# A new opening for a backbone kernel: tokens by rows, the modulation map by quarters

## The chip, the cores and the metric

The kernel runs on 1 core of a Trainium2 chip. The metric is the device time of one execution in microseconds (us). Engines: TensorE (PE; PEld are its weight loads), VectorE (DVE), ScalarE (ACT), GpSimd (POOL) and SyncE (SP), whose queue issues the DMAs.

## The reference

Two layers work on 1024 latent tokens (width 1024) and 256 context tokens. The part that matters here is the start of layer 0: both streams are normalised by their root mean square, then scaled and shifted by numbers that come from a map of the conditioning vector, and projected to q, k and v.

```python
mod = silu_c @ w_mod[i] + b_mod[i]          # 1024 -> 6 x 1024
mod_c = silu_cc @ w_mod[i] + b_mod[i]
sh1, sc1, gt1, sh2, sc2, gt2 = jnp.split(mod[:, None, :], 6, axis=-1)
h = modulate(rmsnorm(x, g_attn[i]), sh1, sc1)       # h * (1 + scale) + shift
hc = modulate(rmsnorm(ctx, g_attn[i]), sh1c, sc1c)
q, k, v = attn_inputs(h, w_in, gq, gk, n_kv)        # y = h @ w_qkv, rmsnorm of q and k per head
```

Behind it come neighbourhood attention, an output projection and a gated ConvFFN, and layer 1 with sliding-window attention; the change does not touch these.

## The kernel before

**Layout.** Activations lie with channels on the partitions, as eight blocks of 128 channels (k = 0 to 7), and tokens along a row. The tokens form chunk 0 (latent 0 to 511, tiles 0 to 3 of 128 tokens), chunk 1 (latent 512 to 1023, tiles 4 to 7) and chunk 2 (context, tiles 8 and 9). Products keep fp32 accuracy by splitting both sides in a hi part and a lo part and adding three products: whi x hi, whi x lo, wlo x hi. A projected tile (128 tokens by 384 columns: q, k and v of one pair of heads) therefore takes 8 blocks x 3 = 24 products. The weights of a head pair come as four slabs j of two channel blocks each; ScalarE makes whi, VectorE wlo.

**Order of work.** Nearly every instruction is issued through one helper (line 51, so most rows of the profile say L51). A planner (`Sched`, lines 61 to 223) holds operations with an engine, an assumed duration, what they read and write, a key and buffer counts; it plays them through and lays down one fixed order for each engine. At run time an engine executes its list in that order and waits in place for whatever an instruction still lacks. Two planners follow each other at the start: `sa` for the opening (lines 791 to 936) and `sc` for layer 0's attention (lines 965 to 1232).

**The opening before.** SP loads the context and chunk 0 (x, channels on partitions), then the shift and scale columns of layer 0's map in eight chunks `wm` of 1 MB, one for each block of input channels; the two accumulators `mod` are complete only when the eighth has landed. Then slabs 0 to 2, chunk 1 and slab 3. Meanwhile the sums of squares are made by ScalarE (`sq`) and VectorE (`nsum`), folded over partitions by a product with a column of 1/D (`nps<-invd,nsum`), raised to the power -1/2 by GpSimd, improved by a Newton step on VectorE, and spread again: VectorE makes diagonal matrices `dg`, a product with ones gives the factor for each token on all partitions (`nps<-dg,ones`), and VectorE multiplies x by it. When the map is complete, ScalarE copies it out (`modsb`), TensorE turns it (`modt`), VectorE adds the bias (`modc`), and `apply` makes the hi and lo parts of chunks 2 and 0 (`h0chi`, `h0clo`, `h0hi`, `h0lo`). Chunk 1 waits: `plan_norm` (lines 636 to 724) does its norm inside `sc`, between the first projections, with its lo parts called `n1lo`.

**The attention of layer 0.** For each of eight head pairs, `plan_na_qkv` (line 977) projects the ten tiles in the order 8, 9, 0 to 7 (`mm`, two PSUM banks). Each tile then has a tail: ScalarE copies the bank to `qraw` (two buffers), squares (`qsq`), splits v; VectorE and GpSimd make the factor of the q and k norm (`qv`, `qy`, `qn`), ScalarE and VectorE the hi and lo parts `st`, TensorE turns them into `pt` (four matrices, and `klt`, the lo parts of k, once for two tiles), ScalarE and VectorE copy out q, kk, kl. `plan_na_su` (line 1092) does the attention of two query tiles and a head: scores `s` (context first), an exponential on ScalarE into `S`, a scale, the turn of S into `pt`, its hi and lo parts (`pthi`, `ptlo`), products with v into `pv`.

Of the kernel before, what the change touches and what calls it, by code (L numbers as in the profile page):

```python
# [19 lines left out]
KT = 8  # L20
# [206 lines left out]
def trunk_kernel(ctx, tc, xperm, xseq, cc, wmod, bmod, gnorm, na_wqkv, na_gq, na_gk, na_bias, na_wo,  # L227
# [111 lines left out]
    def t_act(n):  # L339
        return 0.094 + n / 1200.0  # L340
# [452 lines left out]

    with tc.tile_pool(name="x0", bufs=1, reuse_waits="tile") as xp, \
            tc.tile_pool(name="lw0", bufs=2, reuse_waits="tile") as lw, \
            tc.tile_pool(name="ps0", bufs=1, space=PS, reuse_waits="tile") as ps:
        xs = [hpool.tile([P, KT, 512], F32, tag="hhi", name="x0", bufs=2),
              Parts([lo_part("x1", F32) for _ in range(4)], 2),
              Parts([wring.tile([P, 1024], F32, tag="wlo", name="x2").rearrange("p (k t) -> p k t", k=4) for _ in range(2)], 4)]
        h = [hi_lo("h0", 0), None, hi_lo("h0", 2)]  # L800


        sa = Sched(dict(raw=3, w=WBUFS, sq=2, nsum=1, n=2))
        t_mb = 2.45
        for c, parts, key in ((2, 2, 0), (0, 4, 2), (1, 4, 30)):
            t0, n = CH[c]
            for k in range(0, KT, KT // parts):
                def load(e, c=c, parts=parts, k=k, t0=t0, n=n):
                    src = xperm[:, KT * t0 + k * n:KT * t0 + (k + KT // parts) * n].rearrange("p (k t) -> p k t", t=n)
                    dma.dma_start(xs[c][:, k:k + KT // parts, :] if c == 0 else xs[c].tiles[k * parts // KT], src)  # L810
                sa.op("dma", t_mb * n / parts / 256, load, writes=[("x", c, k + i) for i in range(KT // parts)], key=key + k / KT)
# [3 lines left out]
        accs, raws = [None] * 2, [None] * KT  # L815
        for kt in range(KT):
            def load(e, kt=kt):
                raws[kt] = xp.tile([P, 2, 1024], F32, tag="wm", name=f"wm{kt}", bufs=KT)
                dma.dma_start(raws[kt].rearrange("p v c -> p (v c)"), wmod[0, kt * P:(kt + 1) * P, 0:2 * D])

            def mm(e, kt=kt):
                for v in range(2):
                    if kt == 0:
                        accs[v] = ps.tile([P, 512], F32, tag="mod", name=f"mod{v}", bufs=2)
                    mod_mm(accs[v], kt, raws[kt][:, v, :], kt == 0, kt == KT - 1)
            sa.op("dma", t_mb, load, writes=[("wm", kt)], key=4 + kt)
            sa.op("pe", 0.86, mm, reads=[("wm", kt)], writes=[("acc", v) for v in range(2)], key=0)
        for v in range(2):
            J = {}

            def cp(e, v=v, J=J):
                J["sb"] = xp.tile([P, 256], F32, tag="modsb", name="modsb0", bufs=2)
                act.activation(J["sb"], accs[v][:, :256], AF.Copy)

            def tr(e, v=v, J=J):
                J["gen"] = mod_finish(0, v, J["sb"], lambda: ps.tile([P, 512], F32, tag="modt", name="modt", bufs=2))
                next(J["gen"])

            def fin_(e, J=J):
                for _ in J["gen"]:  # L840
                    pass
            sa.op("act", 0.28, cp, reads=[("acc", v)], writes=[("sb", v)], key=-1)
            sa.op("pe", 0.43, tr, reads=[("sb", v)], writes=[("modt", v)], key=-1)
            sa.op("dve", 0.2 + 0.2 * v, fin_, reads=[("modt", v), ("bmod",), ("gn",)], writes=[("modc", v)], key=-1)

        def stats(c, key):

            n = CH[c][1]
            nt = n // P
            J = {}  # L850
            x = xs[c]
            for k in range(KT):
                def sq(e, k=k):
                    J["s", k] = lw.tile([P, 512], F32, tag="sq" if k else "nsum", name="sq" if k else "nsum", bufs=2 if k else 1)
# [4 lines left out]
                sa.op("act", t_act(n), sq, reads=[("x", c, k)], writes=[("sq", c, k)] if k else [("sums", c)], key=key + k,  # L859
                      acq=[("sq", ("sq", c, k), 1)] if k else [("nsum", ("nsum", c), 1)])  # L860
                if k:
                    sa.op("dve", t_dve(n), add, reads=[("sq", c, k), ("sums", c)], writes=[("sums", c)], key=key + k,
                          rel=[("sq", c, k)])

            def mp(e):
                J["mp"] = ps.tile([P, 512], F32, tag="n", name="nps", bufs=2)
                for i in range(nt):
                    pe.matmul(J["mp"][:, i:i + 1], J["s", 0][:, i * P:(i + 1) * P], invd, start=True, stop=True)
            sa.op("pe", 0.22 * nt, mp, reads=[("sums", c)], writes=[("mp", c)], key=key, acq=[("n", ("mp", c), 1)],
                  rel=[("nsum", c)])  # L870

            def v(e):
                for a in "vyt":
                    J[a] = tiny.tile([P, 4], F32, tag="n" + a, name="n" + a)[:, :nt]
                dve.tensor_scalar(out=J["v"], in0=J["mp"][:, :nt], scalar1=EPS, scalar2=None, op0=ALU.add)
            sa.op("dve", 0.08, v, reads=[("mp", c)], writes=[("v", c)], key=key, rel=[("mp", c)], port=False)
# [9 lines left out]
            def dg(e):  # L886
                J["dg"] = lw.tile([P, 512], F32, tag="sq", name="dg", bufs=2)
# [3 lines left out]
            sa.op("dve", 0.2 * nt, dg, reads=[("y", c)], writes=[("dg", c)], key=key, acq=[("sq", ("dg", c), 1)])  # L891

            def bc(e):
                J["bc"] = ps.tile([P, 512], F32, tag="n", name="nps", bufs=2)
                for i in range(nt):
                    pe.matmul(J["bc"][:, i * P:(i + 1) * P], ones, J["dg"][:, i * P:(i + 1) * P], start=True, stop=True)
            sa.op("pe", 0.22 * nt, bc, reads=[("dg", c)], writes=[("bc", c)], key=key, acq=[("n", ("bc", c), KT)], rel=[("dg", c)])
            for k in range(KT):
                sa.op("dve", t_dve(n), lambda e, k=k: dve.tensor_tensor(
                    out=x[:, k, :], in0=x[:, k, :], in1=J["bc"][:, :n], op=ALU.mult),  # L900
                    reads=[("bc", c)], writes=[("x", c, k)], key=key + 8 + k, rel=[("bc", c)], port=False)
# [1735 lines left out]
```

## Time and profile before

| | us |
|---|---|
| median of 3 runs | 2819.89 |
| lowest, highest run | 2819.53, 2821.8 |
| the profiled execution | 2819.35 |
| its span in the profile | 2817.6 |

The span is the time between the first and the last recorded instruction of the one profiled execution; all single durations below come from that execution. A row of the timeline has the start, the duration, the engine, the line, the operation, the tile that is written and those that are read, partitions x elements, the count, and in brackets the idle time of the engine before it and what ended it. Durations of neighbouring instructions overlap, so the cost of one in a row of many is the distance between starts. A plain fp32 product leaves two records, so a count of 8 there can be four products.

### The profile page before, as it was taken

How to read it: one execution, taken by the hardware profiler on the slowest of the kernel's cores; microseconds unless marked ns; L12 is line 12 of the kernel's file. 1: busy time of each engine (PE TensorE's matmuls, PEld its weight loads, DVE VectorE, ACT ScalarE, POOL GpSimd, SP SyncE). 2: the span in 40 equal slices, each digit the busy share in tenths (PEclk: the TensorE clock that was granted, in tenths of full speed). 3: DMA queues.
4: the chain of work that ended last, by engine and by line, in shares of the span. 5: the costliest groups of instructions: out<-in, count | busy, mean ns of one | idle time of the engine just before them, and what ended most of it. 6: DMA issues, size and time to landing. Idle time of an engine off the chain costs nothing. (4 is left out here: it accounts for less than half of the span.)

```text
span 2817.6 us, 45649 instructions
## 1 busy us (share of the span) xinstructions
PE 2758.1 (98%) x16205; PEld 2427.5 (86%) x16205; DVE 2288.3 (81%) x5013; ACT 1687.3 (60%) x3312; POOL 394.4 (14%) x652
## 2 busy tenths in 40 slices
PE   6999999999999999999999999999999999999999
PEld 5999999999889987777788878999987788888887
DVE  7888878889688687778797788888988888888757
ACT  5877777778456554444454457888864555455443
POOL 1222212223000000000010006455420000000000
PEclk9999999999999999999999999999999999999999
DMA  6232222224645544444376561010263322334745
GB/s 250 64 97 81 72 70 82 89 77 145 238 146 187 185 162 139 153 144 161 135 257 199 172 213 33 13 37 19 81 203 128 124 104 99 113 108 145 252 150 180
DMA packets 144295, 373.54 MB, mean 133 GB/s; under 512 B 22081, under 2 KB 35009, under 8 KB 142657
## 3 DMA queue, kind: packets, MB, share of 16 engines
q1 hardware_dynamic: 144064, 370.60, 39.5%
q8 instruction: 128, 2.10, 0.3%
q14 instruction: 103, 0.84, 0.1%
HBM read 303.50 MB, written 67.04 MB: 132 GB/s over the span
## 5 line engine op out<-in xcount | busy, mean ns | idle before, releaser
L51 ACT ACTIVATE whi<-wraw 128x512 fp32r<-128x512 f32 (+1 forms) x264 | 212.3, 805 | 202.8 <-PE uc L51 62.3
L51 DVE TENSOR_TENSOR wlo<-wraw,whi 128x512 fp32r<-128x512 f32 (+1 forms) x264 | 239.5, 909 | 45.0 <-ACT whi L51 44.5
L51 DVE TENSOR_TENSOR ptlo<-pt,pthi 128x512 fp32r<-128x512 f32 (+2 forms) x384 | 223.4, 596 | 56.3 <-ACT pthi L51 52.4
L51 PE MATMUL dn<-ghi,whi 128*128 128x512 f32 x616 | 243.8, 396 | 0.0
L51 PE MATMUL dn<-ghi,wlo 128*128 128x512 f32 x616 | 242.8, 394 | 0.0
L51 PE MATMUL dn<-glo,whi 128*128 128x512 f32 x616 | 242.0, 393 | 0.0
L51 ACT ACTIVATE S<-S,m 128x640 f32<-128x640 f32 (+3 forms) x288 | 220.6, 767 | 23.1 <-DVE m L51 17.7
L51 ACT ACTIVATE pthi<-pt 128x512 fp32r<-128x512 f32 (+2 forms) x384 | 194.3, 523 | 66.6 <-PE pt L51 58.2
L51 DVE SCALAR_TENSOR_TENSOR u<-c,cv,u 128x1023 f32<-128x1023 f32 x176 | 223.2, 1280 | 6.9 <-ACT u L51 5.8
L51 ACT ACTIVATE whi<-s 128x1024 fp32r<-128x1024 f32 (+1 forms) x120 | 113.2, 943 | 191.3 <-PE uc L51 133.9
L51 ACT ACTIVATE ghi<-graw 128x512 fp32r<-128x512 f32 x154 | 96.5, 631 | 192.5 <-PE dn L51 108.3
L51 PE MATMUL pt<-idr,S 128*128 128x128 f32 x1280 | 193.8, 273 | 3.2 <-DVE ptlo L51 2.0
L51 PE MATMUL mm<-whi,h0hi 128*128 128x384 f32 x512 | 181.6, 355 | 0.4 <-ACT qraw L51 0.4
L51 DVE TENSOR_TENSOR glo<-graw,ghi 128x512 fp32r<-128x512 f32 x154 | 105.6, 689 | 83.8 <-ACT ghi L51 76.1
L51 PE MATMUL mm<-wlo,h0hi 128*128 128x384 f32 x512 | 172.3, 337 | 0.0
L51 DVE TENSOR_TENSOR wlo<-s,whi 128x1024 fp32r<-128x1024 f32 (+1 forms) x120 | 129.7, 1081 | 40.8 <-ACT whi L51 40.7
L51 PEld LDWEIGHTS pt<-idr,S 128*128 128x128 f32 x1280 | 151.0, 140 | 12.1 <-DVE ptlo L51 2.9
L51 POOL TENSOR_TENSOR n1y<-n1v,mhalf 128x4 f32<-128x4 f32 (+1 forms) x9 | 9.2, 1023 | 993.1 <-DVE n1v L51 993.1
L51 PE MATMUL ua<-t12hi,whi 128*128 128x512 f32 x352 | 138.7, 394 | 5.5 <-ACT t12hi L51 4.0
L51 POOL TENSOR_TENSOR qy<-qv,mhalf 128x4 f32<-128x4 f32 (+1 forms) x112 | 119.6, 1068 | 155.6 <-DVE qv L51 136.6
L51 PEld LDWEIGHTS dn<-ghi,wlo 128*128 128x128 f32 x616 | 115.5, 187 | 28.4
L51 PEld LDWEIGHTS dn<-glo,whi 128*128 128x128 f32 x616 | 115.5, 188 | 27.5
(347 smaller groups left out, 8759.3 us busy)
## 6 DMA issues: line engine op xcount, KB each, us to landing
wraw<-in_w_up_dram SPq DMA_DIRECT2D x132, 512.0 KB, 3.5
wm<-in_wmod_dram SPq DMA_DIRECT2D x80, 512.0 KB, 4.2
wraw<-in_w_down_dram SPq DMA_DIRECT2D x44, 512.0 KB, 3.6
graw<-g_dram SPq DMA_DIRECT2D x44, 512.0 KB, 4.4
wraw<-in_w_down_dram SPq DMA_DIRECT2D x88, 256.0 KB, 3.2
graw<-g_dram SPq DMA_DIRECT2D x66, 256.0 KB, 2.8
slab<-in_na_wqkv_dram SPq DMA_DIRECT2D x32, 384.0 KB, 3.8
woraw<-in_na_wo_dram SPq DMA_DIRECT2D x24, 512.0 KB, 4.1
```

The costliest lines, as they stand in the source:

```text
L51: r = f(*a, **k)
```

## The change

1. **Tokens by rows.** Context and chunks 0 and 1 are loaded a second way, as ten tiles `tok` of 128 tokens x 1024 channels (input `xtok`, six buffers). ScalarE squares a tile and sums it along the row in the same instruction, so that VectorE's sums and the product with 1/D go.
2. **Turned and normalised by TensorE.** For chunks 2 and 0 the product of a token block with the diagonal `dg` gives at once the transposed and normalised block in PSUM (`nps` and `pv` in turn); ScalarE or VectorE copies it out. Chunk 1 is also loaded the old way (`xperm`, now only this chunk) and multiplied by a broadcast factor, and its whole norm moves from `sc` into the opening; the part of `plan_norm` for layer 0 is no longer called.
3. **The map by quarters.** The map's columns come in four quarters of 256 channels (two blocks k), each in two 1 MB loads that hold all 1024 input channels. Each quarter is accumulated in one bank, copied, turned and finished by itself, so that `apply` for blocks 2q and 2q+1 needs quarter q alone.
4. **Six tiles in the opening.** For head pair 0 the tiles 8, 9, 0, 1, 2, 3 (`ORDER[:NQ]`) are projected slab by slab as the quarters come, in six PSUM banks: 8 and 9 in `mm`, 0 to 2 in `s`, 3 in `pv`. The attention planner finds these six accumulators done.

The core of the diff:

```diff
+    NQ = 6
+    def first_tag(tt):
+        return "mm" if tt > 7 else "s" if tt < 3 else "pv"
...
-        sa = Sched(dict(raw=3, w=WBUFS, sq=2, nsum=1, n=2))
+        sa = Sched(dict(raw=3, w=WBUFS, n=2, mod=1, tok=6, dg=2, wm=4))
+        t_mb, LATE, K1 = 2.45, 0.5, 40
...
+        def plan_quarter(q):
+            J = {}
+            for hf in range(2):
+                def load(e, hf=hf):
+                    J["raw", hf] = xp.tile([P, 4, 2, 256], F32, tag="wm", name=f"wm{q}", bufs=4)
+                    dma.dma_start(J["raw", hf].rearrange("p k v c -> p (k v c)"),
+                                  wmod0[q, :, 2048 * hf:2048 * hf + 2048])
+                def mm(e, hf=hf):
...
+                    for kt in range(4 * hf, 4 * hf + 4):
+                        for v in range(2):
+                            g = 2 * v + kt % 2
+                            pe.matmul(J["acc"][32 * g:32 * g + 32, :256], cpad[:, kt, :], J["raw", hf][:, kt % 4, v, :],
+                                      start=kt < 2, stop=kt > 5, skip_group_check=True)
...
-            for k in range(KT):
-                def sq(e, k=k):
-                    act.activation(J["s", k][:, :n], x[:, k, :], AF.Square)
-                def add(e, k=k):
-                    dve.tensor_tensor(out=J["s", 0][:, :n], in0=J["s", 0][:, :n], in1=J["s", k][:, :n], op=ALU.add)
+            for i in range(nt):
+                def load(e, i=i):
+                    J["tok", i] = xp.tile([P, D], F32, tag="tok", name="tok", bufs=6)
+                    dma.dma_start(J["tok", i], xtok[i0 + i])
+                def sq(e, i=i):
...
+                    act.activation(junk, J["tok", i], AF.Square, accum_out=J["v"][:, i:i + 1])
...
-            for k in range(KT):
-                sa.op("dve", t_dve(n), lambda e, k=k: dve.tensor_tensor(
-                    out=x[:, k, :], in0=x[:, k, :], in1=J["bc"][:, :n], op=ALU.mult),
+            for k in range(KT):
+                def tr(e, k=k):
+                    J["p", k] = bank()
+                    for i in range(nt):
+                        pe.matmul(J["p", k][:, i * P:(i + 1) * P], J["tok", i][:, k * P:(k + 1) * P], J["dg"][:, i * P:(i + 1) * P],
+                                  start=True, stop=True)
+                sa.op(("act", "dve"), (t_actp(n), t_dve(n)), lambda e, k=k: copy(e, x[:, k, :], J["p", k][:, :n]),
...
+            for tt in ORDER[:NQ]:
+                def mm(e, j=j, tt=tt, c=c):
...
+                    for kt in (2 * j, 2 * j + 1):
+                        wh, wl = [a[:, kt % 2, :] for a in slabs.get(j)]
+                        for i, (a, w) in enumerate(((hh, wh), (hl, wh), (hh, wl))):
+                            pe.matmul(first_acc[tt][:, :384], a[:, kt, sl], w, start=(kt == 0 and i == 0),
+                                      stop=(kt == KT - 1 and i == 2))
...
-        plan_qkv_mm(sc, key, psa, h, tt, slabs, hp, J, 0, ("h0", tt // 4) if hp == 0 else None)
+        if n < NQ:
+            J["acc"] = first_acc[tt]
+            sc.hold(first_tag(tt), I + ("acc",), 1)
+        else:
+            plan_qkv_mm(sc, key, psa, h, tt, slabs, hp, J, 0, ("h0", tt // 4) if hp == 0 else None)
...
-    plan_norm(sc, 0, psa, wk, sums0, xs[1], h[1], 1.0)
```

How the planner then lays the lists down is shown at three places. The first is SP's queue, before from the last loads of x to chunk 1 (`x_114` and on):

```order
L51 DMA x_113<-in_xperm_dram 128x1024 x4
L51 DMA wm_165<-in_wmod_dram 128x2048
L51 DMA wm_180<-in_wmod_dram 128x2048
L51 DMA wm_199<-in_wmod_dram 128x2048
L51 DMA wm_216<-in_wmod_dram 128x2048
L51 DMA wm_244<-in_wmod_dram 128x2048
L51 DMA wm_263<-in_wmod_dram 128x2048
L51 DMA wm_275<-in_wmod_dram 128x2048
L51 DMA wm_297<-in_wmod_dram 128x2048
L51 DMA slab<-in_na_wqkv_dram 128x768 x3
L51 DMA x_114<-in_xperm_dram 128x1024
```
and after, behind six token tiles and slab 0; `wm_183` and `wm_206` are the first quarter, and what each load waits for stands in brackets:

```order
L51 DMA wm_183<-in_wmod_dram 128x2048 [waits DMAHW2_49]
L51 DMA wm_206<-in_wmod_dram 128x2048 [waits DMAHW3_49]
L51 DMA slab<-in_na_wqkv_dram 128x768 [waits DMAHW4_49]
L51 DMA wm_240<-in_wmod_dram 128x2048 [waits DMAHW5_49]
L51 DMA wm_259<-in_wmod_dram 128x2048 [waits DMAHW6_49]
L51 DMA tok<-in_xtok_dram 128x1024 [waits DMAHW7_49,PE_49]
L51 DMA tok<-in_xtok_dram 128x1024 [waits DMAHW0_49,PE_49,Activation_49]
L51 DMA slab<-in_na_wqkv_dram 128x768 [waits DMAHW1_49]
L51 DMA wm_327<-in_wmod_dram 128x2048 [waits DMAHW2_49,PE_49]
L51 DMA wm_356<-in_wmod_dram 128x2048 [waits DMAHW3_49,PE_49]
L51 DMA tok<-in_xtok_dram 128x1024 [waits DMAHW4_49,PE_49,Activation_49]
L51 DMA tok<-in_xtok_dram 128x1024 [waits DMAHW5_49,PE_49,Activation_49]
```
The map is spread out between slabs and chunk 1's token tiles; behind these rows come slab 3, the fourth quarter and then chunk 1 in the old layout. The last two token tiles take the buffers of chunk 0's first tiles, so they wait for TensorE's transposes.

The second is TensorE's list, before around the end of the map:

```order
L51 MATMUL mod_189<-wm_297,cpad 32x256 x4
L51 MATMUL mod_194<-wm_297,cpad 32x256 x4
L51 MATMUL modt<-idr,modsb_329 128x128 x2
L51 MATMUL modt<-idr,modsb_331 128x128 x2
L51 MATMUL mm<-whi,h0chi 128x384
```
and after around the second quarter (`wm_240`, `wm_259`), with the last transposes of chunk 0 and the first products of tile 0:

```order
L51 MATMUL mod<-wm_240,cpad 32x256 x8
L51 MATMUL pv<-dg,tok 128x128 x4
L51 MATMUL mod<-wm_259,cpad 32x256 x8
L51 MATMUL nps<-dg,tok 128x128 x4
L51 MATMUL pv<-dg,tok 128x128 x4
L51 MATMUL s<-whi,h0hi_129 128x384
```
Projections now stand between the quarters. Behind the fourth quarter the list has quarter 2's products of tiles 0 to 3, then the 48 products of the context, with quarter 3's products of tile 0 in their middle and of tiles 1 to 3 at the end.

The third is ScalarE's list around its first exponential, before

```order
L51 ACTIVATE h0hi<-t,modc 128x512 x4
L51 ACT_TABLE_LOAD
L51 ACTIVATE S,sm<-S,m_874 128x256
L51 ACTIVATE S,sm<-S,m_883 128x256
L51 ACTIVATE q<-pt 128x256
```
and after:

```order
L51 ACTIVATE qraw<-pv 128x384
L51 ACT_TABLE_LOAD
L51 ACTIVATE S,sm<-S,m_879 128x256
L51 ACTIVATE qsq<-qraw 128x256
L51 ACTIVATE v<-qraw 128x2x64
L51 ACTIVATE q<-pt 128x256
L51 ACTIVATE S,sm<-S,m_887 128x256
L51 ACTIVATE q<-pt 128x256
L51 ACTIVATE S,sm<-S,m_906 128x256
L51 ACTIVATE S<-S,sm 128x256
L51 ACTIVATE kll<-pt 128x2x256
L51 ACTIVATE S,sm<-S,m_916 128x256
```
The hi parts of chunk 1 are gone from in front of the exponentials, and the tails of tiles 1 to 3 stand between them.

More of the change, by code (lines that the diff above doesn't have):

```diff
@@ L828, in trunk_kernel @@
[L828 to L844, printed above, removed]
@@ L865, in mp @@
[L865 to L870, printed above, removed]
+            for i in range(nt):
[3 more added lines that the diff above has]
+                def sq(e, i=i):
+                    if i == 0:
+                        for a in "vyt":
+                            J[a] = tiny.tile([P, 4], F32, tag="n" + a, name="n" + a)[:, :nt]
+                    junk = lw.tile([P, D], F32, tag="junk", name="junk", bufs=1)
+                    act.activation(junk, J["tok", i], AF.Square, accum_out=J["v"][:, i:i + 1])
+                sa.op("dma", t_mb / 2, load, writes=[("tok", c, i)], key=lkey + 0.1 * i, acq=[("tok", ("tk", c, i), 1 if c == 1 else 1 + KT)])
+                sa.op("act", t_act(D) + 0.2, sq, reads=[("tok", c, i)], writes=[("ss", c)], key=key, rel=[("tk", c, i)])
@@ L872, in v @@
             def v(e):
[L873 to L876, printed above, removed]
+                dve.tensor_scalar(out=J["v"], in0=J["v"], scalar1=1.0 / D, scalar2=EPS, op0=ALU.mult, op1=ALU.add)
+            sa.op("dve", 0.08, v, reads=[("ss", c)], writes=[("v", c)], key=key)
@@ L890, in dg @@
                                       op0=ALU.mult)
[L891 to L897, printed above, removed]
@@ L1231, in trunk_kernel @@
     plan_oproj0()
-    sc.run({e: max(0.0, sa.free.get(e, 0.0) - T0) for e in ("act", "dve", "pool")})
+    sc.run({e: max(0.0, sa.free.get(e, 0.0) - T0) for e in ("pe", "act", "dve", "pool")})
     ph.close()
```

162 lines of the change are left out of this document (106 added, 56 removed).

## The prediction

> **What bounds the kernel now.** I read the page's busy times first, then its forty slices, then the stretches of the first 300 us, then the timeline at the places where a stretch shows idle time. The first two lines are engine sums and TensorE's busy tenths; in the stretches the columns are length, then busy time (and instructions) of PE, PEld, DVE, ACT and POOL, then the granted clock, the DMA share and GB/s.
>
> ```profile
> PE 2758.1 (98%) x16205; PEld 2427.5 (86%) x16205; DVE 2288.3 (81%) x5013; ACT 1687.3 (60%) x3312; POOL 394.4 (14%) x652
> ...
> PE   6999999999999999999999999999999999999999
> ```
> ```profile
> 0.00:37.90 37.90, 15.55 (x156) 7.97 (x156) 20.93 (x60) 14.04 (x26) 2.43 (x8) 0.93 0.97 378
> 37.90:42.90 5.00, 4.97 (x15) 4.81 (x16) 5.00 (x16) 5.00 (x11) 0.00 (x0) 0.51 1.04 387
> 42.90:69.50 26.60, 26.27 (x160) 25.26 (x159) 23.84 (x70) 18.01 (x45) 8.78 (x10) 1.00 0.16 51
> 69.50:101.30 31.80, 29.02 (x190) 26.55 (x189) 30.24 (x96) 27.62 (x69) 10.84 (x15) 1.00 0.11 28
> 101.30:300.00 198.70, 198.70 (x1464) 192.33 (x1463) 165.90 (x594) 146.75 (x384) 44.98 (x64) 1.00 0.27 85
> ```
> TensorE is the bound: 98% busy, and without a gap from 101 to 300 us. Only the first slice is poor. Up to 37.9 us TensorE does 15.6 us of work, none of it a projection; then it works 5 us at half clock (0.51); then it idles 2.8 us between 69.5 and 101.3. From there on a microsecond won earlier is a microsecond won at the end, since the queue behind stays full.
>
> What holds the first projection back is the modulation map. The two chunks that landed last, the turn of the finished map and the first projection:
>
> ```profile
> 30.09 1.07 PE L51 MATMUL mod<-wm,cpad 128*32 128x256 f32 x16 [1.42 <-DMA wm<-in_wmod_dram]
> 33.09 1.93 PE L51 MATMUL mod<-wm,cpad 128*32 128x256 f32 x16 [1.93 <-DMA wm<-in_wmod_dram]
> 35.22 1.11 PE L51 MATMUL modt<-idr,modsb 128*128 128x128 f32 x4 [0.19 <-ACT modsb L51]
> 37.93 0.66 PE L51 MATMUL mm<-whi,h0chi 128*128 128x384 f32 x1 [1.60 <-DVE h0chi L51]
> ```
> and the DMA rate of the first 120 us in forty slices of 3 us:
>
> ```profile
> GB/s 78 289 396 427 425 423 421 412 429 410 394 409 408 381 300 129 5 0 3 0 61 70 0 5 0 0 3 0 0 0 44 62 29 249 317 162 25 179 173 0
> ```
> The transfers run without a break from 6 to 42 us, so the opening is bound by bytes first.
>
> **The change, part by part.**
>
> *Landing times.* Summed, the slices give 4.85 MB at 15 us, 11.13 at 30, 14.76 at 39. In before, 11.6 MB stand in the queue up to the last map chunk, which is 31.2 us by that sum; TensorE saw it at 33.1, so a landing is seen 1.9 us after its bytes. In the new queue six token tiles, a slab and the quarter itself (5.8 MB) stand up to the end of the first quarter, 8.3 MB to the second, 11.8 to the third and 15.3 to the fourth. By the same sum they are seen at 19.1, 25.0, 33.6 and 42.4 us. The last quarter comes 9 us later than the last chunk did, since chunk 1's tokens (2.1 MB, which are now read twice) and the four slabs stand ahead of it. In exchange the first quarter comes 14 us earlier.
>
> *The hold in the queue.* The token loads behind the third quarter wait until the last transposes of chunk 0 free their buffer, and slab 3 and the fourth quarter are queued behind them on SP. The third quarter's bytes keep the engines busy to 31.7 us, and the transposes end at about 29 (the start of 17.7 found below, then 6.5 of transposes, four bursts and a turn): nothing is lost if a load starts to move within 2.7 us. The first load of before shows about that:
>
> ```profile
> 0.73 0.39 SPq L51 DMA_DIRECT2D x<-in_xperm_dram  x1
> ...
> 4.58 0.42 ACT L51 ACTIVATE nsum<-x 128x256 f32<-128x256 f32 x1 [2.57 <-DMA x<-in_xperm_dram]
> ```
> It is issued at 0.73 and used at 4.58; its 0.52 MB at some 0.4 MB/us are 1.3 of these 3.85 us. Later than that, each microsecond of hold is one of the end.
>
> *TensorE's queue in the opening.* The rows that price it, at full clock unless said:
>
> ```profile
> 48.68 0.33 PE L51 MATMUL mm<-whi,h0hi 128*128 128x384 f32 x1
> ...
> 51.11 0.34 PE L51 MATMUL mm<-wlo,h0hi 128*128 128x384 f32 x1
> ...
> 66.98 1.05 PE L51 MATMUL pt<-S,ones 128*128 128x128 f32 x8
> 67.79 0.42 PE L51 MATMUL mm<-whi,h0hi 128*128 128x384 f32 x1
> ```
> The first two are the ends of 15 products in a row: 14 steps in 2.43 us, 0.1735 each for a product of 384 columns. A plain fp32 128x128 product takes 0.81/4 = 0.20 us (it is two records). A map burst is 1.07 us and one turn half of 1.11, about 0.5 (rows above). The order of after then gives: chunk 0's transposes 32 x 0.20 = 6.5; eight bursts 8.6; four turns 2.0; the broadcast for chunk 1 0.8; six tiles 144 x 0.1735 = 25.0. That is 42.9 us. It can start when chunk 0's norm is known: its last token tile is seen at about 13.2 us (3.3 MB), ScalarE's square of 128x1024 takes about 1.05, and then come the steps of the norm, taken from these rows
>
> ```profile
> L51 ACT ACTIVATE whi<-s 128x1024 fp32r<-128x1024 f32 x88 | 93.3, 1060 | 183.3 <-PE uc L51 133.9 <-issue 35.3 <-PE ua L51 5.2
> ```
> ```profile
> 20.57 1.01 POOL L51 TENSOR_TENSOR ny<-nv,mhalf 128x4 f32<-128x4 f32 x1 [8.04 <-DVE nv L51]
> ...
> 24.12 0.88 DVE L51 TENSOR_SCALAR dg<-idr,ny 128x128 f32<-128x128 f32 x4
> ```
> 1.0 for the power, 0.6 for Newton, 0.9 for the diagonals, hops of 0.2 to 0.3 between: 17.7 us. So TensorE's own queue ends at 17.7 + 42.9 = 60.6, and about 1.4 us of waits on VectorE's lo parts of chunk 2 and on the broadcast make it **62.1**. The landing gives nearly the same: after 42.4 come the burst (1.1), the turn (0.5) and the products ordered behind it, 24 of quarter 2, 48 of context and 24 of quarter 3 (96 x 0.1735 = 16.7), 60.7 and 0.9 of wait. VectorE has 17 us of work between 43.4 and 60 (chunk 1's scale and lo parts among it, 16 x 0.7), just under that. So three bounds meet at 60 to 62 and I take 62.1 for the end of six tiles, with -1 and +2.5 as ends.
>
> *What before has done at the same mark.* Six tiles are done there at 69.46, and the first product of the second head pair starts at 101.27:
>
> ```profile
> 69.46 0.46 PE L51 MATMUL pt<-idr,st 128*128 128x128 f32 x4
> 69.76 0.35 PE L51 MATMUL s<-kkc,q 128*128 128x256 f32 x1
> ...
> 70.82 0.44 PE L51 MATMUL mm<-whi,h0hi 128*128 128x384 f32 x1
> ```
> ```profile
> 101.27 0.35 PE L51 MATMUL mm<-whi,h0chi 128*128 128x384 f32 x1
> ```
> Between them are 31.8 us with 2.8 idle, so 29.0 of work. After has the same stretch, with two turns of q/k and one of k-lo more (0.3 + 0.3 + 0.45, which before did among the six tiles) and two score products fewer (-0.35): 29.7 us. Chunk 1's norm (two steps of TensorE, 1.7 us) is gone from the main phase and already counted. Without new waits the second head pair would start at 62.1 + 29.7 = 91.8: 9.5 us earlier.
>
> *The new wait.* Six tiles now end together, so ScalarE and VectorE get six tails at once. I walk ScalarE by the slots between these starts:
>
> ```profile
> 64.68 0.61 ACT L51 ACTIVATE klc<-pt 128x512 fp32r<-128x512 f32 x1
> 65.21 0.49 ACT L51 ACTIVATE qraw<-mm 128x384 f32<-128x384 f32 x1
> 65.60 0.41 ACT L51 ACTIVATE st<-qn 128x256 fp32r<-128x256 f32 x1
> 65.90 0.41 ACT L51 ACTIVATE qsq<-qraw 128x256 f32<-128x256 f32 x1
> 66.21 0.30 ACT L51 ACTIVATE st<-qn 128x128 fp32r<-128x128 f32 x1
> ```
> ```profile
> 79.49 1.28 ACT L51 ACT_TABLE_LOAD   x1
> 80.78 0.51 ACT L51 ACTIVATE S<-S,m 128x256 f32<-128x256 f32 x1
> ```
> After 62.1 TensorE has 27 products (4.7), then the two q/k turns of the context with three products behind each and the k-lo turn: 68.7; ScalarE's klc is done at 69.6. Then its order has two qraw (0.39 each), four st (0.3, 0.2), a qsq (0.31) and a v (0.2), 2.3 us; the table load 1.28; three exponentials (0.5), one scale (0.5), a qsq, a v, two q (0.27), 3.0: it releases the second S at 76.2. TensorE, with nine products (1.6), the scores (1.06), six products (1.0) and the turns of tiles 0 and 1 (0.95), is there at 73.3 and has nothing else in its order: 3.1 us lost. The next product of its row is of P hi, which waits for kll, the fourth exponential and pthi (0.5 each, 77.7): 1.2 more, and 0.3 for the tile behind it. That is 4.6 us, where before lost 2.8. In before the same S transposes had 12 us of products ahead of them. Later waits I take as none: ScalarE's remaining tails run to about 91, TensorE gets there at 93 or later. The ends for this term are 2 (the planner's products cover most of it) and 10 (every tail is late, ScalarE becomes the bound up to the second head pair).
>
> *Sum.* 62.1 + 29.7 + 4.6 = 96.4 against 101.3: **4.9 us gained**. The profiled execution took 2819.4 (span 2817.6 and 1.8 around it), 0.5 under the median of the three runs. 2819.4 - 4.9 = 2814.5, and 2815.0 on the median's scale. A fifth of a per cent, about what a measurement of this kernel can tell from no change, is 5.6 us: the forecast lies just inside.
>
> **Rule and row on the clock.** These two stretches show how the clock was lost:
>
> ```profile
> 32.00:34.00 2.00, 0.91 (x12) 0.45 (x16) 0.00 (x0) 0.00 (x0) 0.00 (x0) 0.64 1.01 396
> 34.00:36.00 2.00, 1.81 (x16) 0.83 (x8) 1.01 (x2) 1.95 (x4) 0.00 (x0) 0.50 1.04 414
> ```
> Bursts of 1.07 us with gaps of 1.42 and 1.93 (the rows above) were enough for it to fall. In my walk no gap is over 1 us from 18 us on, so I take full clock; but each quarter is a place where a late landing could open such a gap, and the half clock keeps a chance. [...]
>
> **The rivals.**
>
> - *Dear tails.* The six tails cost about 9 us, since each of my slots has a hop less than the chip. For it: ScalarE is busy 27.6 of 31.8 us in that stretch now, and VectorE 30.2. Against: VectorE loses chunk 1's sixteen steps there (about 11 us). Time 2819.
> - *Cheap tails.* TensorE loses 1 to 2 us only, or the opening ends at 60.6: 2811 or less. Against: the table load is on the path and the order shows no product behind it.
> - *Slower: half clock in the opening.* If the short waits between quarters keep the clock at 0.5 up to the last quarter, a product costs 0.33 us in place of 0.1735 (row of 37.9 to 42.9: 15 products in 5 us), 72 products 11.3 us more and six bursts (1.93 against 1.07) 5.2: with TensorE's queue full nothing hides these 16.5, and the time is 2831. The gain is a loss from 31 products at half clock on. Against: the walk has TensorE busy nearly throughout.
> - *The quarters don't lead.* The transposes of chunk 0 end later than 31 us, SP holds the fourth quarter, and the opening ends with the hold: 2 us of delay give 2817, 5 give 2820. I count it with the dear tails.
>
> **How the numbers follow.** Forecast (2811.5 to 2817.5) 0.60; dear tails or a held queue (2817.5 to 2823) 0.20; cheap tails 0.12; half clock 0.08. Of the forecast's share somewhat under half lies below 2814.3, so faster by over 0.2% is 0.12 + 0.28 = 0.40, slower 0.08, within 0.52. The range 2810 to 2822 leaves out the half clock and the ends of the two neighbours, together under 0.2.
>
> **What would show it.** In the profile of after: the burst of the fourth quarter at 42 to 43 us; the first product of quarter 0 at 27 to 29; granted clock 1.0 from 20 us on; the six tiles done at 61 to 64.5; two idle times of TensorE of about 3 and 1 us near 73 to 78, on S and pthi; the first product of the second head pair at 95 to 98; no idle behind it to 300 us. A clock of 0.5 between 28 and 44, a fourth quarter later than 44, or idle time of over 8 us between 62 and 96 would make the forecast wrong.

## The result and the profile after

| | before | after |
|---|---|---|
| median, us | 2819.84 (22 runs) | 2815.24 (22 runs) |
| lowest, highest | 2818.57, 2824.09 | 2812.12, 2818.66 |
| the profiled execution | 2819.35, span 2817.6 | 2817.0, span 2815.2 |

The ratio is 0.9983, with a 95% interval of 0.9976 to 0.9989: faster by 4.6 us, where 4.9 was forecast. That is under the 5.6 us (0.2%) that the forecast named as its line. The profiled execution gained only 2.4; why is part of what follows.

The page of after has TensorE's sum and its tenths:

```profile
PE 2763.7 (98%) x16273; PEld 2437.3 (87%) x16273; DVE 2280.8 (81%) x5005; ACT 1689.7 (60%) x3310; POOL 390.5 (14%) x652
...
PE   8999999999999999999999999999999999999999
```
The first slice went from 6 to 8. The stretches of after, in the same columns as those of before (length; busy time of PE, PEld, DVE, ACT, POOL; granted clock; DMA share; GB/s):

```profile
18.00:28.00 10.00, 9.45 (x106) 7.15 (x102) 6.37 (x17) 4.44 (x8) 0.00 (x0) 1.00 1.02 415
28.00:44.00 16.00, 15.83 (x136) 12.59 (x128) 11.28 (x36) 10.85 (x20) 1.01 (x1) 1.00 1.02 413
44.00:62.00 18.00, 16.63 (x107) 15.51 (x106) 16.96 (x36) 9.63 (x18) 0.00 (x0) 1.00 0.54 189
70.00:80.00 10.00, 6.70 (x48) 6.14 (x48) 7.53 (x37) 9.51 (x28) 5.41 (x9) 0.96 0.01 2
80.00:90.00 10.00, 10.00 (x53) 9.78 (x53) 7.48 (x27) 6.66 (x21) 3.39 (x5) 0.70 0.04 13
100.00:300.00 200.00, 200.00 (x1488) 193.21 (x1487) 169.82 (x598) 149.20 (x388) 47.02 (x68) 1.00 0.27 85
```
From 18 us on TensorE is busy at full clock, between the quarters too: the opening does what it says. Then two things show. Between 70 and 80 TensorE idles 3.3 us. And between 80 and 90 it is busy all the time, yet gets through 53 records in place of the 73 or so of a full stretch, at a granted clock of 0.70. From 100 on it has no gap.

TensorE's timeline has the marks of the forecast: first product of quarter 0, burst of the fourth quarter, first product behind the six tiles, the three waits, two neighbours at half clock, the first product of head pair 2.

```profile
30.39 0.42 PE L51 MATMUL s<-whi,h0hi 128*128 128x384 f32 x1
...
44.61 1.07 PE L51 MATMUL mod<-wm,cpad 128*32 128x256 f32 x16 [0.25 <-DMA wm<-in_wmod_dram]
...
64.03 0.33 PE L51 MATMUL mm<-whi,h0hi 128*128 128x384 f32 x1
...
77.08 0.54 PE L51 MATMUL pt<-idr,klt 128*128 128x128 f32 x4 [1.83 <-DVE kkl L51]
78.25 0.63 PE L51 MATMUL pt<-idr,S 128*128 128x128 f32 x4 [0.63 <-DVE sm L51]
79.71 0.80 PE L51 MATMUL pv<-pthi,v 128*128 128x256 f32 x2 [0.84 <-ACT pthi L51]
...
80.82 0.52 PE L51 MATMUL mm<-whi,n1lo 128*128 128x384 f32 x1
81.14 0.52 PE L51 MATMUL mm<-wlo,h0hi 128*128 128x384 f32 x1
...
98.49 0.33 PE L51 MATMUL mm<-whi,h0chi 128*128 128x384 f32 x1
```
The six tiles are done at 64.03 (69.46 in before): 5.4 us gained. Head pair 2 starts at 98.49 (101.27): 2.8 are left. The stretch between the marks grew from 31.8, with 2.8 of waits in it, to 34.5. After has three waits of 1.83 + 0.63 + 0.84 = 3.3 us there, and the products behind them stand 0.32 apart (80.82, 81.14) instead of 0.1735. They do so up to 85.9.

What makes the first wait is read on ScalarE and VectorE:

```profile
73.89 1.28 ACT L51 ACT_TABLE_LOAD   x1
75.18 0.51 ACT L51 ACTIVATE S<-S,m 128x256 f32<-128x256 f32 x1
...
76.19 0.36 ACT L51 ACTIVATE q<-pt 128x256 fp32r<-128x256 f32 x1
```
```profile
75.81 0.16 DVE L51 RECIPROCAL sm<-sm 128x1 f32<-128x1 f32 x1 [0.50 <-ACT S L51]
...
76.61 0.41 DVE L51 CAST kkl<-pt 128x256 fp32r<-128x256 f32 x1
```
TensorE's next turn (k lo) needs a `pt` bank. Both are held by the turned tiles 0 and 1, each until ScalarE has copied out its q and VectorE its kk (`kkl`). Tile 0's bank comes free first: its q is copied from 76.19 on, its kk from 76.61 to 77.02, and the turn starts at 77.08. In VectorE's list that copy stands behind the reciprocal of the first exponential's sum, which waits 0.50 us for ScalarE, and in ScalarE's list this exponential stands behind the table load.

In this execution the transfers also start slower than in some others. The DMA rates of the first 120 us (slices of 3 us) show it, after first, then a relative with the same opening (the run fill10 below):

```profile
GB/s 113 226 285 386 429 415 434 408 397 430 411 407 423 401 411 379 309 283 26 0 0 0 0 0 0 0 8 0 0 44 0 66 146 333 273 20 0 131 219 8
```
```profile
GB/s 109 246 408 410 435 399 436 399 422 408 412 410 421 403 410 375 370 101 0 0 0 0 0 0 0 8 0 0 44 47 146 152 308 182 3 16 297 45 49 60
```
At 12 us after has 0.49 MB less ((408 + 410 + 246 + 109 - 113 - 226 - 285 - 386) x 3 us = 489 kB), 1.2 us at 0.41 MB/us; the fourth quarter's burst comes 2.1 us later in it. But fill10 is the quickest of the relatives. By the same sum after moved 3.03 MB by 12 us, fill10 3.52, and after's second profile and the other four relatives with this opening 3.15 to 3.22. Against these five after is 0.3 to 0.5 us late by its bytes, yet its six tiles end 1.0 to 1.4 us later; the rest is not explained.

### The profile page after: what moved, and what is told of

It reads as the page before. It is cut to its first block, busy times and chain, and to the rows that moved or that the text cites. A ratio compares the mean times of both kernels' runs of the same rounds, so it can differ in the third digit from the quotient of the medians.

```text
span 2815.2 us, 45755 instructions
## 1 busy us (share of the span) xinstructions
PE 2763.7 (98%) x16273; PEld 2437.3 (87%) x16273; DVE 2280.8 (81%) x5005; ACT 1689.7 (60%) x3310; POOL 390.5 (14%) x652
## 5 line engine op out<-in xcount | busy, mean ns | idle before, releaser
L51 PE MATMUL mm<-whi,h0hi 128*128 128x384 f32 x480 | 170.8, 356 | 0.0
L51 PE MATMUL mm<-wlo,h0hi 128*128 128x384 f32 x480 | 161.9, 337 | 0.0
L51 PE MATMUL ua<-t12lo,whi 128*128 128x512 f32 x352 | 138.2, 393 | 0.9 <-DVE t12lo L51 0.9
```

Source lines behind the costliest of these rows:

```text
L51: r = f(*a, **k)
```

## The experiments

**The theory** after the result: the gain comes from the products between the quarters; the six tails at once give part of it back, as a wait that hangs on the table load and then as a half clock that this wait brings. **The rivals:** the gain is the norm's or chunk 1's; the waits hang on the tails' own chain; the half clock has another cause.

| run | median, us (runs) | ratio to before, 95% interval |
|---|---|---|
| exp_early | 2805.46 (5) | 0.9946, 0.9933 to 0.9958 |
| exp_early_before | 2810.77 (6) | 0.9968, 0.9956 to 0.9980 |
| fill10 | 2812.15 (7) | 0.9974, 0.9963 to 0.9984 |
| quarters_late | 2818.07 (11) | 0.9994, 0.9985 to 1.0003 |
| pad32 | 2806.07 (5) | 0.9950, 0.9938 to 0.9963 |
| exp_alias | 2813.50 (11) | 0.9978, 0.9970 to 0.9987 |
| nq4 | 2817.08 (11) | 0.9990, 0.9981 to 0.9999 |
| tok_late | 2819.53 (11) | 0.9996, 0.9987 to 1.0005 |
| pad32_before | 2810.88 (5) | 0.9964, 0.9950 to 0.9977 |
| best | 2803.15 (5) | 0.9939, 0.9927 to 0.9952 |
| after_again | 2816.07 (8) | 0.9986, 0.9976 to 0.9996 |

**quarters_late: no product between the quarters.**

```diff
-        stats(1, 16, 10)
         apply(2, 28)
         apply(0, 28.5)
+        stats(1, 16, 10)
...
-                sa.op("pe", 6 * t_pe(384), mm, reads=[("wl", j), ("h", c, 2 * j), ("h", c, 2 * j + 1)], writes=[("qa", tt)],
+                sa.op("pe", 6 * t_pe(384), mm, reads=[("wl", j), ("h", c, 2 * j), ("h", c, 2 * j + 1), ("acc", 3)], writes=[("qa", tt)],
```


> The changed kernel, but all 144 products of the six tiles stand behind the fourth quarter's burst (one more condition in the plan; chunk 1's norm is planned behind the two others so that its buffers come free in order). If the gain comes from the products between the quarters: TensorE idles from about 37 to 44 us, the six tiles are done at 71 to 73 instead of 64.0, head pair 2 starts at 103 to 106, the time 2820 to 2823, no gain left. If the gain is the norm's or chunk 1's: within 1.5 us of 2815.

The time is 2818.07, and the gain over before can no longer be told from none. Its stretches, then its marks on TensorE:

```profile
28.00:44.00 16.00, 8.73 (x79) 3.90 (x77) 12.94 (x40) 9.32 (x19) 1.43 (x1) 0.72 1.02 414
44.00:62.00 18.00, 18.00 (x101) 17.36 (x94) 12.98 (x29) 6.92 (x11) 0.00 (x0) 0.87 0.45 166
```
```profile
42.69 1.94 PE L51 MATMUL mod<-wm,cpad 128*32 128x256 f32 x16 [0.48 <-DMA wm<-in_wmod_dram]
...
73.31 0.41 PE L51 MATMUL mm<-whi,h0hi 128*128 128x384 f32 x1
...
101.19 0.33 PE L51 MATMUL mm<-whi,h0chi 128*128 128x384 f32 x1
```
The six tiles end at 73.31, 9 us later than in after, as this theory wanted. Head pair 2 starts at 101.19, earlier than the 103 to 106 expected, but at this mark nothing is left of the gain over before (101.27). The price in time is 2.8 us by the medians, whose intervals just overlap, and not the 5 to 8 expected: with a TensorE that arrives later its tails no longer wait (no gap from 60 to 110 us). So most of the gain, 2.8 of 4.6 us, comes from the products between the quarters, and their full price shows only together with the waits that they bring. (The plan behind the opening differs in places too, so that the 2.8 us are not of the opening to the last tenth.) The run also shows the forecast's third rival at work: without products between them the bursts from 32 us on take 1.47 to 1.94 us and the clock from 28 to 44 is 0.72.

**fill10: needless products in the first wait.** Ten products into an idle bank, right behind the turn of tile 1; nothing else moves.

```diff
+        if n == 3:
+            def fill(e):
+                a = psa("pv", F32)
+                for i in range(10):
+                    pe.matmul(a[:, :384], h[0][0][:, 0, 0:P], slabs.get(0)[0][:, 0, :], start=True, stop=True)
+            sc.op("pe", 0.0, fill, reads=[K("pt")], writes=[("fill",)], key=-50, acq=[("pv", ("fill",), 1)], rel=[("fill",)])
```


> The changed kernel with ten needless products (10 x 0.17 us, into the idle bank pv) in TensorE's list right behind the turn of tile 1, where TensorE waits 1.83 us; nothing else changes place. If the half clock of 79 to 86 us comes of that gap: the clock stays full, the stretch 80 to 86 is about 3 us shorter, head pair 2 at 95.5, the time 2812. If the two later gaps (0.63 and 0.84) are enough for the clock to fall: no change, 2815. If VectorE's and ScalarE's tails hold TensorE there anyway: clock full, but the 3 us come back as waits, under 1 us gained.

Its stretch from 80 to 90 and its rows on TensorE:

```profile
80.00:90.00 10.00, 10.00 (x76) 9.90 (x75) 9.67 (x37) 8.86 (x26) 3.88 (x6) 1.00 0.10 27
```
```profile
61.91 0.33 PE L51 MATMUL mm<-whi,h0hi 128*128 128x384 f32 x1
...
72.97 2.00 PE L51 MATMUL pv<-whi,h0hi 128*128 128x384 f32 x10
...
76.14 0.63 PE L51 MATMUL pt<-idr,S 128*128 128x128 f32 x4 [0.63 <-DVE sm L51]
77.61 0.50 PE L51 MATMUL pv<-pthi,v 128*128 128x256 f32 x2 [0.84 <-ACT pthi L51]
...
93.91 0.34 PE L51 MATMUL mm<-whi,h0chi 128*128 128x384 f32 x1
```
The two later waits are the same to the hundredth, and the clock is 1.00 (76 records against 53). From the first `pv` product to head pair 2 it takes 93.91 - 77.61 = 16.30 us, in after 98.49 - 79.71 = 18.78: the half clock costs 2.5 us, and without the first gap it does not come. (This is one profile, of the quickest of the seven runs.) Against after the median is 3.1 us lower, but the intervals of the two ratios overlap. The stretch between the marks, 32.0 against 34.5, is the firmer number.

**exp_early: the table load out of the way.** An exponential of two columns behind the opening's SiLU.

```diff
     act.activation(cpad[:, :, 0:2], cpad[:, :, 0:2], AF.Silu)
+    early = cpool.tile([P, 2], F32, name="early")
+    act.activation(early, cpad[:, 0, 0:2], AF.Exp)
```


> One tiny exponential right behind the SiLU of the conditioning vector, so that the exponential's table load (1.28 us at 73.89 in the changed kernel) moves to about 9 us, where ScalarE has an idle time of 1.6; no other instruction changes place. If TensorE's waits of 76 to 80 us (1.83, 0.63, 0.84) hang on that load: 1 to 1.3 us less wait, the first product of head pair 2 at 97.2 instead of 98.49, and if the shorter wait also keeps the clock full behind it, at about 94.5; the time 2811 to 2814. If the tails' own chain (the power on GpSimd, VectorE's steps) sets these waits: no change, 2815.

The first wait went from 1.83 to 1.25 and the second from 0.63 to 0.28, but the time fell by 9.8 us, far more than either theory had. The control said at once that this was not the tails:

**exp_early_before: the same line in the kernel before.**

> The same early exponential in the kernel before, where the table load (1.28 us at 79.49) had 12 us of products on TensorE beside it. If the load costs only where TensorE has nothing else: no change, within 0.7 us of 2819.8. If a load costs its length wherever it stands: 1.3 us less.

Also 9 us, against both theories. Head pair 2 starts there at 101.11 (101.27 without the line), so the opening is no quicker, and the gain must lie far behind it. What the two runs share is the small tile: it shifts most of the tiles allocated after it by 32 bytes in each partition. Two runs take the tile and the exponential apart.

**pad32: the tile without the exponential.**

```diff
+    early = cpool.tile([P, 2], F32, name="early")
+    dve.memset(early, 0.0)
```


> The changed kernel with the two-column tile of the early exponential, but no exponential: the tile is only cleared once at the start. It moves the same tiles by the same 32 bytes in each partition as the run with the early exponential did, and nothing else. If the placement made the products with 512 columns quicker (0.2247 us each instead of 0.2299 in 1500 to 1690 and 2620 to 2800 us): 5 to 7 us less than the changed kernel, 2808 to 2810, with the first 100 us as they were (head pair 2 at 96 to 98.5). If the early table load did all of it: 2815.

2806.07: the shift alone makes nearly all of it. A stretch of layer 1's down projection (`dn`, products with 512 columns), in after and then in pad32:

```profile
2690.00:2730.00 40.00, 40.00 (x174) 32.30 (x174) 22.09 (x34) 15.98 (x27) 0.00 (x0) 1.00 0.44 135
```
```profile
2690.00:2730.00 40.00, 40.00 (x179) 33.11 (x178) 23.53 (x37) 15.94 (x27) 0.00 (x0) 1.00 0.54 169
```
TensorE is busy throughout and at full clock in both, yet 40 us hold 179 products instead of 174. By the distance of their starts a product takes 0.227 us in place of 0.232 (the first and the last start 40.35 us apart over 178 steps in pad32, 40.15 over 173 in after). The first 100 us are as in after: waits of 1.83, 0.62 and 0.69, a clock of 0.80 behind them, 62.60 to 96.77 between the marks (34.2).

**pad32_before: the tile in the kernel before.**

> The kernel before with the small tile of the run with the moved placement, cleared once and never read: the same 32 bytes of shift, no exponential. If the placement is a matter of its own: 512-column products at 0.2247 us, the time about 2811, as in the kernel before with the early exponential (2810.8), head pair 2 at 101.2, and the change itself is again worth 4 to 6 us against the changed kernel with the shift (2806.1). If the early exponential made the 9 us there: 2820.

2810.88, as in the kernel before with the exponential. So the placement is a matter of its own, and in the other placement the change is worth the same: 2810.88 - 2806.07 = 4.8 us. Head pair 2 was expected at 101.2 and starts at 102.91; the profiled execution, 2813.24, is the slowest of the five.

**exp_alias: the exponential without a new tile.**

```diff
-    dsh = spool.tile([P, 104], F32, name="dsh")[:, :8]
+    dshf = spool.tile([P, 104], F32, name="dsh")
+    dsh = dshf[:, :8]
...
+    act.activation(dshf[:, 8:10], cpad[:, 0, 0:2], AF.Exp)
```


> The changed kernel with the early exponential written into spare columns of a tile that is there already, so that no tile moves: the table load alone. If the load is on the path of the tails and the placement is the rest: head pair 2 starts 32 to 32.5 us after the six tiles are done (34.5 in the changed kernel), 512-column products at 0.2299 as before, the time 2812 to 2813.5. If the load does all: 2805.5. If only the placement counts: 2815.

The time is in the range given. TensorE's waits in it, and the marks:

```profile
62.92 0.33 PE L51 MATMUL mm<-whi,h0hi 128*128 128x384 f32 x1
...
75.40 0.53 PE L51 MATMUL pt<-idr,klt 128*128 128x128 f32 x4 [1.25 <-DVE kkl L51]
76.21 0.63 PE L51 MATMUL pt<-idr,S 128*128 128x128 f32 x4 [0.28 <-DVE qt L51]
77.59 0.50 PE L51 MATMUL pv<-pthi,v 128*128 128x256 f32 x2 [0.75 <-ACT pthi L51]
...
93.91 0.33 PE L51 MATMUL mm<-whi,h0chi 128*128 128x384 f32 x1
```
The load is worth 3.3 - 2.3 = 1.0 us of waits in this profile. The other 2.3 us stay without it, so the larger part of the waits hangs on the tails' own chain, as the second rival has it: the copy `kkl` that the k-lo turn waits for now starts at 74.93, at the end of a row of VectorE's work that has no gap from 72.0 on. Behind the waits the clock stayed full (1.00 from 80 to 90), and the stretch is 31.0, under the 32 to 32.5 expected and 34.5 in after. In exp_early the waits were the same 1.25, 0.28 and 0.75, and there the clock fell in part (0.87 from 70 to 80, 0.96 from 80 to 90; 32.2 between the marks). So with waits of this size the clock fell in one of the two profiles. Over all runs 2813.50 can't be told from after's 2815.24 by the intervals.

**nq4: four tiles in the opening.** `NQ = 6` becomes `NQ = 4`.

> The changed kernel with four tiles (8, 9, 0, 1) in the opening instead of six; tiles 2 and 3 are projected behind it. If the products between the quarters are the gain: 24 fewer stand ahead of the fourth quarter, so TensorE idles 4.2 us more there; against it, four tails come at once instead of six, and the waits of 76 to 80 (3.3 us) and the half clock behind them (about 2.5) shrink or go. Both together: 2814 to 2819, most likely 2816. If the tails' waits cost more than the products bring: under 2813.

2817.08, as the first theory had it. TensorE's gaps of over 1 us in its opening from 30 us on:

```profile
35.09 1.07 PE L51 MATMUL mod<-wm,cpad 128*32 128x256 f32 x16 [1.08 <-DMA wm<-in_wmod_dram]
41.18 1.07 PE L51 MATMUL mod<-wm,cpad 128*32 128x256 f32 x16 [2.50 <-DVE ny L51]
...
50.71 0.69 PE L51 MATMUL mm<-whi,h0clo 128*128 128x384 f32 x1 [3.19 <-DVE h0clo L51]
```
The idle time comes back in the opening, while of the tails' waits one of 0.43 us is left: the same bargain from the other side, 1.8 us to the worse by the medians, with intervals that overlap.

**tok_late: the fourth quarter ahead of chunk 1's tokens.** `stats(1, 16, 10)` becomes `stats(1, 16, 17)`, planned behind the two `apply` as in quarters_late.

> The changed kernel with chunk 1's token loads queued behind the fourth quarter instead of between the third and fourth (2.1 MB, 5.1 us at 0.415 MB per us); its norm is planned behind the other two so that its buffers come free in order. The fourth quarter's burst should come at 37 to 38 us. If TensorE's queue and not the landing bounds the opening: no change, 2814 to 2816. If the landing of the last quarter bounds it: the six tiles are done 1 to 2 us earlier, 2813. If chunk 1's norm becomes late for tile 4: new waits at 62 us of 2 to 4 us, 2817 to 2819.

The burst comes at 37.94, as expected, and the time is the worst of all runs, 2819.53, just above the range of the third case. The waits on TensorE behind the opening, in their order, then ScalarE ahead of the first of them:

```profile
62.19 0.45 PE L51 MATMUL mm<-whi,h0hi 128*128 128x384 f32 x1 [2.21 <-ACT qraw L51]
...
79.53 0.75 PE L51 MATMUL pt<-idr,klt 128*128 128x128 f32 x4 [2.46 <-DVE kkl L51]
81.01 1.08 PE L51 MATMUL pt<-idr,S 128*128 128x128 f32 x4 [0.73 <-DVE sm L51]
82.78 0.79 PE L51 MATMUL pv<-pthi,v 128*128 128x256 f32 x2 [0.69 <-ACT pthi L51]
```
```profile
60.38 1.38 ACT L51 ACTIVATE h0hi<-x,modc 128x512 fp32r<-128x512 f32 x2 [1.92 <-DVE x L51]
61.67 0.85 ACT L51 ACTIVATE qraw<-mm 128x384 f32<-128x384 f32 x2
```
The six tiles end at 60.0 (62.19 less the wait), 3 to 4 us earlier than in after and its repeat. The first wait is the one that the third case named: chunk 1 is late for tile 4. Tile 4 needs a bank of the context tiles, ScalarE's copy of it (`qraw`) stands behind chunk 1's last hi parts, and these wait for VectorE's work on chunk 1. The waits further on, in the tails, no case named: with three between (0.44, 0.63 and 0.17) all add up to 7.3 us, and the clock is 0.62 from 80 to 90. The earlier landing of the map was worth nothing here, since chunk 1 and the tails did not follow. As its plan differs from after's in more than this queue, the 4.3 us are not the queue's alone.

**best: all three.** exp_early, and seven needless products where fill10 had ten.

> The changed kernel with the early exponential in its own small tile (so with the shift too) and seven needless products (1.2 us) behind the turn of tile 1, where it waits 1.25 us. If clock, table load and placement add up: the clock stays full behind the turn, head pair 2 starts 31 us after the six tiles, the time 2803 to 2804.5, under the 2805.5 of the same kernel without the seven products. If the products delay the k-lo turn: 2806 or more.

2803.15, under both kernels by 16.7 and 12.1 us; under exp_early by 2.3, where the intervals overlap. The clock from 80 to 90 is 1.00, and between the marks (62.84 and 93.72) are 30.9 us. Some 9 us of the gain are the placement and have nothing to do with the change. What a third buffer for `qraw` would bring, for which ScalarE waits 3.45 us up to 66.21 in after, was not tried.

**after_again: a second profile of after.**

> The changed kernel itself once more, for a second profile. If its profiled execution had a slow start of the transfers by chance: six tiles done near 62.5 instead of 64.0 (61.9 to 62.9 in four relatives with the same opening), the stretch behind it again 34 to 34.5 us with the half clock in it, head pair 2 at about 96.8. If the slow start belongs to the kernel: again 64 and 98.5.

```profile
43.64 1.07 PE L51 MATMUL mod<-wm,cpad 128*32 128x256 f32 x16 [0.27 <-DMA wm<-in_wmod_dram]
...
63.04 0.33 PE L51 MATMUL mm<-whi,h0hi 128*128 128x384 f32 x1
...
97.31 0.33 PE L51 MATMUL mm<-whi,h0chi 128*128 128x384 f32 x1
```
The first mark is 1.0 us earlier than in after's first profile and half a microsecond later than the 62.5 expected, so 1.0 us of the late end of the opening there is chance of the execution, and the rest may belong to the kernel. The stretch is again 34.3, with the same waits (1.84, 0.63 and 0.83) and a clock of 0.77 behind them.

## Why the prediction was right, step by step

**Right, with the mechanism that it gave.** The opening ends earlier, the six tails give part of it back, TensorE's queue behind carries the rest to the end. The stretch between the marks was forecast as 29.7 + 4.6 = 34.3 and is 34.5, 34.3 and 34.2 in the three profiles without an added edit there (after, after_again, pad32). But this agreement is luck in its size, made of three errors that cancel:

- *The waits.* Forecast 4.6, measured 3.3. The places were right: with the opening's 1.9 us of delay taken off, S is turned at 76.3 (forecast 76.4) and the first `pv` product starts at 77.8 (77.7). What I had missed is that the first wait falls on a `pt` bank and k lo's turn, so that some of TensorE's work lies between the waits. It ends with a copy of VectorE's, and my walk went by ScalarE alone. The table load is on the path as forecast, for 1.0 us of its 1.28.
- *The work between the marks.* Forecast 29.7; after's 34.5 less 3.3 of waits and 2.5 of half clock is 28.7. The row of before from which I worked it out may carry slower first products behind its own waits; which instructions the 1.0 us is made of was not taken apart.
- *The clock: the step that failed.* "In my walk no gap is over 1 us from 18 us on, so I take full clock", says the forecast. The walk of the tails, a few lines above, had a gap of 3.1 us in it. The half clock that follows costs 2.5 us, shown by fill10. I had priced it as a rival for the opening alone, where it did not come.

**The opening.** Forecast 62.1; 64.0 and 63.0 in after, 61.9 to 62.9 in the five relatives with the same opening. The landings were forecast at 19.1, 25.0, 33.6 and 42.4; in fill10 the bursts start at 18.6, 25.7, 34.3 and 42.5. TensorE's sum of work was nearly right: 42.9 forecast, 44.2 of busy time in after from 17.72 (the first burst) to 64.03. What I had not allowed for is the spread between executions: TensorE's first transposes start between 9.85 (fill10) and 11.14 us (exp_alias). The start does not decide alone when the opening ends, since exp_alias starts last and ends at 62.9.

**The signs named ahead.** The six tiles, the queue without idle time behind 100 us and the full clock in the opening came as named. The fourth quarter's burst did not: at 44.61 it lies outside 42 to 43 and past the 44 that was to speak against the forecast (43.64 in after_again, 42.5 to 43.8 in the five relatives). The first product of quarter 0 came at 30.39 instead of 27 to 29, and head pair 2 at 98.49 (97.31 in after_again) instead of 95 to 98. The profiled execution of after was a late one, and the half clock was not in the forecast.

**The held queue.** SP issues chunk 1's last token loads only at 30.03, and the rate in that slice is still 411 GB/s: no transfer was late for it, as forecast.

**Half clock in the opening.** Not in after (1.00 from 18 to 62). quarters_late shows that it was a real risk (0.72 from 28 to 44, bursts of up to 1.94 us), and that it is the products between the quarters that keep it away.

**The gain in time.** Forecast 4.9, measured 4.6 by the medians and 4.8 in the other placement. The profiled executions show only 2.4, for two reasons. The first is the late end of the opening in that execution. The second lies far behind, at the end of layer 1's attention, where before's profile kept its clock and after's lost it (before, then after):

```profile
2040.00:2060.00 20.00, 18.13 (x111) 14.74 (x112) 19.78 (x49) 16.09 (x36) 11.24 (x18) 1.00 0.61 191
```
```profile
2040.00:2060.00 20.00, 17.29 (x96) 14.52 (x95) 19.02 (x46) 16.62 (x35) 7.82 (x11) 0.91 0.49 159
```
In fill10 and pad32 the same stretch has 1.00, in exp_early 0.91, in after_again 0.94. So the loss does not come in every execution of an opening like this one. But both profiles of after itself have it and the three of kernels with the old opening (before, exp_early_before, pad32_before: 1.00 each) do not; whether the change makes it more likely is not shown.

**Waits and the clock.** In after, after_again and pad32 waits of 1.83, 0.63 and 0.84 (1.84, 0.63 and 0.83 in after_again; 1.83, 0.62 and 0.69 in pad32), with only turns between them, were enough for the clock to fall: 0.70, 0.77 and 0.80 from 80 to 90. From the last product ahead of the first wait to the first `pv` product are 5.3 us in these three, 4.2 in exp_early and exp_alias and 2.6 in fill10; in these last three, in that order, the clock from 80 to 90 is 0.96, 1.00 and 1.00. In before it fell, to 0.64 from 32 to 34 and 0.50 from 34 to 36, with a burst of map products between the gaps of 1.42 and 1.93. The same gaps of 1.25, 0.28 and 0.75 brought it down in one profile (exp_early, 0.87 from 70 to 80) and not in another (exp_alias, 1.00), though these two kernels also differ in placement. So in these profiles the gaps alone do not settle it, and what the turns between the waits do to the clock is not shown.

## What to carry to other kernels

Where a landing opens work for several consumers, count the tails that will come due together: the gain of an earlier landing ends where their engine can't follow, and what it gives back is the wait and the half clock behind the wait (here 5.4 us won at the end of the six tiles, 2.8 left at head pair 2). Waits of a microsecond or two that one puts into a forecast should carry a chance and a price for the clock too (2.5 us here). And before a gain of a few microseconds is put down to an edit, run a control that moves the same tiles by the same bytes and does nothing else.

## What the hardware showed that was not expected

- **Placement.** A shift of most tiles by 32 bytes in each partition made both kernels 9 us faster (2819.8 to 2810.9, 2815.2 to 2806.1). In the stretch shown, 512-column products of the down projection take 0.227 us in place of 0.232, with TensorE busy throughout and the clock at 1.00. Which operand's address matters was not tried, nor whether these products make up all of the 9 us.
- **The clock behind waits.** Three waits of 3.3 us in all within 4.5 us, with only turns between them, brought half clock for about 6 us in after (0.50 from 80 to 86), at a cost of 2.5. Ten useless products in the first of them kept it full (1.00 from 70 to 90 in fill10).
- **The load of the exponential's table** takes 1.28 us where it stands late (73.89 in after) and early (9.20 in exp_alias). Once early it serves: with squares, copies and scales behind it, no other load comes before the first exponential (72.31 in exp_early, 72.65 in exp_alias), and the one at 73.89 is gone.
